# Three products of 512 columns where there were two of 512 and two of 256, on weight parts placed 64 bytes further

## The chip, the cores and the metric

One core of one Trainium2 chip runs the kernel. The time is device time of one execution, in microseconds (us). Three runs of the kernel before gave 994.24, 994.9 and 995.12 us; their median is 994.9 us.

## The reference, cut to what matters

Two layers of a decoder trunk on a sequence of 256 positions and 1024 features, all float32. Each layer is a gated feed-forward network, a mixer, and a second feed-forward network:

```python
x = x + 0.5 * swiglu(rms_norm(x, ffn1_norm), ffn1_w_gate_up, ffn1_w_down)
h = rms_norm(x, mix_norm)
z = h @ w_in                      # u, q, k, v and two gates
y_pool = multiscale_pool(u, pool_w, pool_scale)
y_attn = moba_attention(q, k, v)  # q and k normed by head, with rotary positions
merged = gates[:, :, 0] * (y_pool @ w_branch_pool) + gates[:, :, 1] * (y_attn @ w_branch_attn)
x = x + merged @ w_out
x = x + 0.5 * swiglu(rms_norm(x, ffn2_norm), ffn2_w_gate_up, ffn2_w_down)
```

Nearly all of the work is in the products of activations with weights: 1024 by 5632 and 2816 by 1024 in each feed-forward network, 1024 by 4096 in `w_in`, and three smaller ones in the mixer.

## The kernel before, in words

**Products in parts.** Every float32 operand is split into two float32r parts, a high one and a low one (`hi` and `lo` of the weights; for activations the two stand beside each other in one tile). A product of two operands is then three products of parts: high by high, high by low, low by high. In this text a step is one block of 128 rows in the sum over features.

**Two ways to lay a product on TensorE.** In most of the kernel the weights are stationary: a block of 128 by 128 of `hi` is loaded, and 512 columns stream past it (the high and the low part of the activations for 256 positions), then the block of `lo` is loaded and 256 columns stream (the high part alone). `chain` writes such a pair of one 512-column and one 256-column product. In the mixer's branches and its last projection, and in the last eighth of the last network, `chain3` writes three of 256 columns.

In two functions the activations are stationary and the weights stream, so that the result has positions, not features, on the partitions. `tokens` (L686) makes q, k and v in this way: it is called three times a layer, and a call takes two units of weights, two halves of 128 positions, and four steps each, 16 steps in all. `by_tokens` (L555) makes a part of the first product of the three later feed-forward networks. That part goes by sums of quadrants of the operands with seven products instead of eight (`SUMS`, the forms "1" to "7" in `seven`); a form is one unit of weights and four steps. The list `TWO` has two groups of seven such forms, `THREE` has three groups and is used twice, so there are 8 groups and 56 forms. The stationary activations are blocks of `hx` for the forms "1", "2" and "4", and of a tile `sf` with their sums and differences for "3", "5", "6" and "7".

A step in these two functions has four products. `ah` and `al` are the high and low parts of a stationary block, `wh` and `wl` the high and low parts of 512 columns of weights, S is 256:

- 512 columns: `ah` with `wh`
- 256 columns: `ah` with the first half of `wl`
- 512 columns: `al` with `wh`
- 256 columns: `ah` with the second half of `wl`

For the forms "1", "2" and "4" in `by_tokens` the second and the third are exchanged. The same four add into one result of 512 columns.

**How columns are read.** `steps` (L218) reads the streaming operand in four rounds: in each round 4 elements (16 bytes) out of every 16 (64 bytes). The result is written in the same order. All products are recorded on one line, that of `mm` (L110); they are told apart by their tiles.

**Where the operands lie.** A unit of weights is one megabyte, and `buffers` (L202) takes one `raw` tile and two `hi` and two `lo` tiles of 1024 elements each (4096 bytes a partition). There are four `raw` buffers and six each of `hi` and `lo`; the six of one name lie behind one another. Tiles of a multiple of 128 bytes keep the same residue modulo 128 throughout, so `hi`, `lo`, `hx` and the other tiles of parts share one. The tile `sf` (L533) is longer than its content and begins SHIFT, 16 elements or 64 bytes, further in, so it is 64 bytes off the weights that stream past it.

**What sets the order.** SP's queue brings the weights in the order of a plan written out by hand; `unit` takes the next pair of parts and `fetch` (L134) starts the next unit: a DMA into `raw`, the high part by ACT (L209, or L198 for units made of quadrants, in `sum_form`, L187), and the low part by DVE (L210 or L199). A `raw` buffer comes free when DVE has read it, a part's buffer when TensorE has read it. POOL's queue makes sums of quadrants in memory beforehand. TensorE runs its products in the order in which they are written (`keep`). The first six units of each layer's `w_in` (q, k and v, two each) are those that `tokens` takes.

Of the kernel before, what the change touches and what calls it, by code (L numbers as in the profile page):

```python
# [19 lines left out]
F32R = mybir.dt.float32r  # L20
# [5 lines left out]
P = 128  # L26
D = 1024
S = 256
L = 2
NK = D // P  # L30
DFF = 2816
NF = DFF // P
# [6 lines left out]
HALF = 8 * P  # L39
# [6 lines left out]
LU = FU + NF + NF // 2  # L46
GROUPS = {"A": 12, "B": 8, "C": 18}
XF = 2
SHIFT = 16
# [29 lines left out]
def trunk_kernel(ctx: ExitStack, tc: tile.TileContext, x_in, w_in, pw_in, qkn_in, rope_in, mask_in, band_in, out):  # L79
# [4 lines left out]
    parts = ctx.enter_context(tc.tile_pool(name="parts", bufs=6))  # L84
# [24 lines left out]
    def mm(*args, **kw):  # L109
        return keep(nc.tensor.matmul(*args, **kw))  # L110
# [17 lines left out]
    def unit():  # L128

        if not ahead:  # L130
            fetch()
        return ahead.pop(0)

    def fetch(last=None):  # L134

        u = next(plan)
        if isinstance(u, tuple):
            ahead.append(sum_form(*u))
            return
        raw, hi, lo = buffers()  # L140
        n = HALF if u < 4 else 2 * HALF
        for c in range(0, 2 * HALF, n):
            nc.sync.dma_start(raw[:, c:c + n], w_in[u, :, c:c + n])
        for h in range(2):
            low = split(raw[:, h * HALF:(h + 1) * HALF], hi[h], lo[h])
        if last:
            behind(low, last)
        ahead.append((hi, lo))
# [3 lines left out]
    def quadrant(base, g, q):  # L152

        n, kh = base + GROUPS[g] + (0 if q[1] == "1" else 2), int(q[0]) - 1
        return w_in[n:n + 2, :, kh * HALF:(kh + 1) * HALF].rearrange("u p c -> p u c")

    def two_rows(z):
        return z.rearrange("p (i c) -> p i c", i=2)
# [28 lines left out]
    def sum_form(base, n):  # L187

        f, g = n
        z, hi, lo = buffers()  # L190
        src = quadrant(base, g, RAW[f]) if f in RAW else two_rows(far.pop((f, g, base)))
        z = two_rows(z)
        nc.sync.dma_start(z, src)
        z = z.rearrange("p i (k c) -> p i k c", c=2 * P)
        for h in range(2):
            a = z[:, :, 2 * h:2 * h + 2, :]
            hv, lv = (t[h].rearrange("p (k i c) -> p i k c", i=2, c=2 * P) for t in (hi, lo))
            act(hv, a, AF.Copy)  # L198
            tt(lv, a, hv.bitcast(F32), op=OP.subtract)  # L199
        return hi, lo  # L200

    def buffers():  # L202
        raw = raws.tile([P, 2 * HALF], F32, name="raw", tag="raw")
        hi = [parts.tile([P, HALF], F32R, name="hi", tag="hi") for _ in range(2)]
        lo = [parts.tile([P, HALF], F32R, name="lo", tag="lo") for _ in range(2)]
        return raw, hi, lo

    def split(w, hi, lo):
        act(hi, w, AF.Copy)  # L209
        return tt(lo, w, hi.bitcast(F32), op=OP.subtract)  # L210

    def blk(z, b, n=1):

        size = z[0].shape[-1]
        c = b * P % size
        return z[b * P // size][:, c:c + n * P]

    def steps(z):  # L218

        if len(z.shape) == 3:  # L220
            z = z.rearrange("p a s -> p (a s)")
        return z.rearrange("p (s a c) -> p a s c", a=4, c=4)

    def prod(ps, w, xk, first, last, **kw):

        return mm(steps(ps), lhsT=w, rhs=steps(xk), start=first, stop=last, **kw)
# [35 lines left out]
    def behind(z, other):  # L262

        tc.add_manual_dep(z.ins, other.ins.name, mybir.DependencyInfo(
            mybir.DependencyClass.NoSync, mybir.DependencyReason.DATA), reason="behind")
# [46 lines left out]
    hx = acts.tile([P, NK, 2, S], F32R, name="hx")  # L312
# [83 lines left out]
    def eight(dtype, name, at=0):  # L396
        z = acts.tile([P, NK * GW + 4 * SHIFT], dtype, name=name, tag="gates")[:, at:]
        return [z[:, i * GW:(i + 1) * GW] for i in range(NK)]
# [21 lines left out]
    def ffn(after, n0=0, end=False, col=None, base=0, far_at=(), steps_at=()):  # L420
        gs, gt = {}, {}

        def room(name, n0, m):
            g = acts.tile([P, m, 2, S], F32R, name=name, tag=name)
            gt[name] = g
            gs.update({n0 + i: g[:, i] for i in range(m)})
# [9 lines left out]
        abs_, more = {}, []  # L436
# [59 lines left out]
        else:  # L496
# [24 lines left out]
            sf = {}  # L521
# [3 lines left out]
            def x_forms():  # L525

                late = drained[-1]
                for k in range(NK):
                    behind(act(xg[:, k, :], x[:, k, :], AF.Copy, scale=gain[:, l_of[0], col + k:col + k + 1]), late)
                (a11, a21), (a12, a22) = ([z[:, :, t * P:(t + 1) * P] for t in range(2)] for z in (xg[:, :4], xg[:, 4:]))  # L530
                s1, s2 = (pre[:, (8 + 2 * i) * S:(10 + 2 * i) * S].rearrange("p (k s) -> p k s", s=P) for i in range(2))
                s3, s4 = (vt[:, i, :].rearrange("p (k s) -> p k s", s=P) for i in range(2))
                fs = iter(eight(F32R, "sf", SHIFT))  # L533

                def parts_of(n, z):
                    sh, sl = (next(fs).rearrange("p (k s) -> p k s", s=P) for _ in range(2))
                    act(sh, z, AF.Copy)
                    tt(sl, z, sh.bitcast(F32), op=OP.subtract)
                    sf[n] = [(sh[:, k, :], sl[:, k, :]) for k in range(4)]

                tt(s3, a11, a21, op=OP.subtract)
                parts_of("7", s3)
                yield
                tt(s1, a22, a21, op=OP.subtract)
                stt(s2, s1, -1.0, a11, op0=OP.mult, op1=OP.subtract)
                parts_of("6", s2)
                yield
                parts_of("5", s1)
                yield
                stt(s4, s2, -1.0, a12, op0=OP.mult, op1=OP.subtract)  # L550
                parts_of("3", s4)
                room("gb", 16, NF - 16)
                yield

            def by_tokens(f, ps, first):  # L555

                hi, lo = unit()
                more = {} if first else {"skip_group_check": True}
                for k, (ah, al) in enumerate(sf[f]):
                    wh, wl = blk(hi, 4 * k, 4), blk(lo, 4 * k, 4)  # L560
                    low = ps[:, :S], ah, wl[:, :S], False, False
                    prod(ps, ah, wh, first and k == 0, False, **more)
                    if f not in "124":
                        prod(*low, **more)
                    prod(ps, al, wh, False, False, **more)
                    if f in "124":
                        prod(*low, **more)
                    prod(ps[:, S:], ah, wl[:, S:], False, k == 3, **more)
                fetch()

            def gated(c, t, n, sign):
# [54 lines left out]
            for n in FEED[base][2:]:  # L626
                next(xf, None)
                if isinstance(n, str):
                    (turned if n[0] == "t" else seven)(*((int(n[1]), n[2]) if n[0] == "t" else n))
                    continue  # L630
                n, t = n if isinstance(n, tuple) else (n, None)
                pair(unit(), wide(n), *([lambda: turned(int(t[1]), t[2]), NK // 2] if t else ()))
                fetch()
                if n in steps_at:
                    go_on()
                if n == XF:
                    xf = x_forms()
                    for _ in xf if not three else "":
                        pass
                if n % 2 and n > 1:  # L640
                    post(wait[0])
                    wait = [n - 1, n]
# [5 lines left out]
        for f, k in order:  # L648
            u, c = divmod(f * NF + k, 16)
# [4 lines left out]
            hi, lo = parts_of[u]  # L654
            if k == 0:
                sums_of[f] = quarter("ps")
            ps = sums_of[f]
# [28 lines left out]
    def tokens():  # L686

        pt = pmm.tile([P, 2, GW], F32, name="pt", tag="mm")
        for kh in range(2):
            hi, lo = unit()  # L690
            for t in range(2):
                ts = slice(t * P, (t + 1) * P)
                for kk in range(4):
                    k = kh * 4 + kk
                    wh, wl = blk(hi, 4 * kk, 4), blk(lo, 4 * kk, 4)
                    prod(pt[:, t], hx[:, k, 0, ts], wh, k == 0, False)
                    prod(pt[:, t, :S], hx[:, k, 0, ts], wl[:, :S], False, False)
                    prod(pt[:, t], hx[:, k, 1, ts], wh, False, False)
                    prod(pt[:, t, S:], hx[:, k, 0, ts], wl[:, S:], False, k == NK - 1)
        return pt  # L700

    def normed(pt, rt, name):
# [91 lines left out]
    def mix(l, after):  # L794
# [235 lines left out]
        for step in ((0, 0, 6), (1, 0, 6), (2, 0, 6), (0, 6), (1, 6), (2, 6), *((f,) for f in range(3, NK))):  # L1030
            project(*step)

    w3 = [buffers() for _ in range(3)]
    parts3 = eight(F32R, "p3", 2 * SHIFT)
    w3.append((raws.tile([P, 2 * HALF], F32, name="raw", tag="raw"), parts3[:4], parts3[4:]))
    done = 0
    for f in range(0, NK, 2):
# [3 lines left out]
        for u, (raw, hi, lo) in enumerate(w3):  # L1041
            nc.sync.dma_start(raw[:, 2 * f * P:2 * (f + 2) * P], w_in[u, :, 2 * f * P:2 * (f + 2) * P])
            n = 1 if f == 0 else 2
# [114 lines left out]
```

## Time and profile before

| What | Value |
|---|---|
| Median of three runs | 994.9 us (994.24 to 995.12) |
| Span of the profiled execution | 991.9 us |
| Instructions | 16162, of them 6296 matmuls |
| TensorE busy | 986.1 us, 99% |
| VectorE (DVE) busy | 811.2 us, 82% |
| ScalarE (ACT) busy | 661.6 us, 67% |
| DMA moved | 285.19 MB, 288 GB/s on average |
| Granted clock of TensorE | 0.999 |

The page gives the span of the profiled execution, from its first instruction to its last, and no total of its own beside it; the runs of the table lie 2.3 to 3.2 us above that span. A row of the groups has the line, the engine and operation, what is written and read, the shape and the count; behind the first bar the busy time and the mean time of one in ns, behind the second the engine's idle time just before. A row of the timeline has the start and the duration in us. A row of the chain of waits has the start and the length of a piece in us, its engine and line, and the number of instructions in it. PE is TensorE's matmul, PEld its weight load. Matmuls overlap, so the time that one takes from the next is the distance of their starts and not their duration.

### The profile page before, as it was taken

Reading aid. Unit: us, or ns where it says so; the run is one execution under the profiler, and the core shown is the slowest. Engines: PE = TensorE matmul, PEld = TensorE weight load, DVE = VectorE, ACT = ScalarE, POOL = GpSimd, SP = SyncE. Lnnn points to the kernel's source line nnn. Section 1 sums busy time; section 2 is a strip of 40 time slices with the busy share of each in tenths; the row PEclk is TensorE's granted clock in tenths of the full one; section 3 lists DMA queues with packets and bytes.
Section 4 is the critical chain, followed back from the end, with each engine's and each line's share of the span. In section 5 each row is a group of like instructions: output and inputs, shape, how many; then the busy total and the mean of one; then the engine's idle time right before and its main releaser. Section 6 shows DMA issues by size and latency. Waiting matters only on the chain.

```text
span 991.9 us, 16162 instructions
## 1 busy us (share of the span) xinstructions
PE 986.1 (99%) x6296; PEld 895.4 (90%) x6296; DVE 811.2 (82%) x1154; ACT 661.6 (67%) x988; POOL 71.0 (7%) x111
## 2 busy tenths in 40 slices
PE   9999999999999999999999999999999999999998
PEld 8989888898899988889888889988988998888897
DVE  6987777698978798886779999776988887999872
ACT  7865555567766787775578877555677568887641
POOL 0000010104100000000000000000141000000000
PEclk9999999999999999999999999999999999999999
DMA  8889899989979769899979989898799998988840
GB/s 298 322 297 323 254 327 343 309 241 292 323 237 328 255 242 324 297 325 286 311 267 305 321 289 347 277 311 279 258 298 372 248 306 299 320 314 292 293 150 22
DMA packets 50269, 285.19 MB, mean 288 GB/s; under 512 B 4753, under 2 KB 6033, under 8 KB 27409
## 3 DMA queue, kind: packets, MB, share of 16 engines
q1 hardware_dynamic: 36624, 217.05, 58.8%
q0 software_dynamic: 13568, 67.11, 27.7%
q8 instruction: 49, 0.80, 0.3%
q14 instruction: 28, 0.22, 0.1%
HBM read 283.10 MB, written 68.16 MB: 354 GB/s over the span
## 4 chain that ended last, share of the span: by engine, by line
PE 99%; DMA 0%; DVE 0%; ACT 0%; SPq 0%; issue 0%
PE ps L110 68%; PE b L110 15%; PE pt L110 7%; PE two L110 4%; PE pe L110 1%; PE sc L110 1%; PE pt L780 1%; PE y L110 1%; PE b L588 0%; DMA raw<-w 0%; PE tp L736 0%; PE pt L588 0%; PE st L110 0%; PE ss L110 0%; DVE t L681 0%; ACT hi L209 0%
## 5 line engine op out<-in xcount | busy, mean ns | idle before, releaser
L210 DVE TENSOR_TENSOR lo<-raw,hi 128x1024 fp32r<-128x1024 f32 (+2 forms) x303 | 360.9, 1203 | 104.3 <-ACT hi L209 102.9
L209 ACT ACTIVATE hi<-raw 128x1024 fp32r<-128x1024 f32 (+2 forms) x303 | 310.6, 1033 | 194.8 <-PE ps L110 123.1
L110 PE MATMUL ps<-hx,hi 128*128 128x512 f32 x1184 | 400.2, 384 | 0.6 <-ACT hi L209 0.6
L110 PE MATMUL ps<-hx,lo 128*128 128x256 f32 x1184 | 323.7, 273 | 0.0
L110 PEld LDWEIGHTS ps<-hx,hi 128*128 128x128 f32 x1184 | 222.2, 188 | 40.7 <-ACT hi L209 0.8
L110 PEld LDWEIGHTS ps<-hx,lo 128*128 128x128 f32 x1184 | 222.5, 188 | 0.3 <-DVE lo L210 0.3
L199 DVE TENSOR_TENSOR lo<-raw,hi 128x1024 fp32r<-128x1024 f32 x112 | 135.0, 1220 | 17.7 <-ACT hi L198 17.5
L198 ACT ACTIVATE hi<-raw 128x1024 fp32r<-128x1024 f32 x112 | 117.5, 1056 | 41.4 <-PE ps L110 25.3
L110 PE MATMUL ps<-ga,hi 128*128 128x512 f32 (+1 forms) x264 | 87.8, 378 | 0.0
L110 PE MATMUL b<-hi,sf 128*128 128x512 f32 x256 | 87.4, 383 | 0.0
L183 POOL DMA_DIRECT2D f<-w x48 | 44.6, 932 | 557.7 <-DVE ab L259 239.4
L110 PE MATMUL b<-lo,sf 128*128 128x256 f32 x256 | 70.2, 274 | 0.0
L110 PE MATMUL ps<-ga,lo 128*128 128x256 f32 x256 | 69.9, 273 | 0.0
L110 PE MATMUL ps<-gb,hi 128*128 128x512 f32 (+1 forms) x198 | 65.4, 376 | 0.0
L110 PE MATMUL pt<-hi,hx 128*128 128x512 f32 x192 | 64.9, 384 | 0.0
L110 PE MATMUL b<-hi,hx 128*128 128x512 f32 x192 | 59.1, 388 | 0.0
L110 PEld LDWEIGHTS ps<-ga,hi 128*128 128x128 f32 x264 | 49.0, 188 | 8.2
L110 PEld LDWEIGHTS b<-hi,sf 128*128 128x128 f32 x256 | 48.0, 188 | 8.4
L110 PE MATMUL pt<-lo,hx 128*128 128x256 f32 x192 | 52.5, 274 | 0.0
L110 PE MATMUL ps<-gb,lo 128*128 128x256 f32 x192 | 52.4, 273 | 0.0
L110 PEld LDWEIGHTS ps<-ga,lo 128*128 128x128 f32 x256 | 48.1, 188 | 0.0
L110 PEld LDWEIGHTS b<-lo,sf 128*128 128x128 f32 x256 | 48.0, 188 | 0.0
(209 smaller groups left out, 1590.6 us busy)
## 6 DMA issues: line engine op xcount, KB each, us to landing
raw<-w SPq DMA_DIRECT2D x168, 1024.0 KB, 7.2
f<-w POOLq DMA_DIRECT2D x48, 1024.0 KB, 11.9
raw<-f SPq DMA_DIRECT2D x32, 1024.0 KB, 5.8
raw<-w SPq DMA_DIRECT2D x16, 256.0 KB, 5.3
out_dram<-gx SPq DMA_DIRECT2D x8, 128.0 KB, 1.9
gx<-x SPq DMA_DIRECT2D x3, 256.0 KB, 5.5
qk<-pw SPq DMA_DIRECT2D x2, 256.0 KB, 5.7
gx<-x SPq DMA_DIRECT2D x1, 300.0 KB, 2.8
```

Source lines behind the costliest of these rows:

```text
L110: return keep(nc.tensor.matmul(*args, **kw))
L183: z = nc.gpsimd.dma_start(two_rows(far[f, g, base]), src, **kw)
L198: act(hv, a, AF.Copy)
L199: tt(lv, a, hv.bitcast(F32), op=OP.subtract)
L209: act(hi, w, AF.Copy)
L210: return tt(lo, w, hi.bitcast(F32), op=OP.subtract)
L780: keep(nc.tensor.transpose(pt[:, h, o * P:(o + 1) * P], pr[:, h, c * P:(c + 1) * P], ident))
```

## The change

In `by_tokens` and `tokens` each step has three products of 512 columns: `ah` with `wh`, `al` with `wh`, `ah` with `wl`. The two halves of `wl` are no longer apart, and all forms have the same order. The sums are the same.

Each `hi` and `lo` tile gets 2 x SHIFT more elements (128 bytes a partition). The parts of the units that stream in these two functions (all of `sum_form`, and the first six units of each layer's `w_in`) start 64 bytes into their tiles, the others at the start. The content of `sf` starts 128 bytes into its tile, so it stays 64 bytes off those weights; `hx` stays where it was, so it is now 64 bytes off them too.

```diff
@@ fetch
-        raw, hi, lo = buffers()
+        t = (u - NF - NF // 2) % LU
+        raw, hi, lo = buffers(SHIFT if t < 6 else 0)
@@ sum_form
-        z, hi, lo = buffers()
+        z, hi, lo = buffers(SHIFT)
@@
-    def buffers():
+    def buffers(at=0):
         raw = raws.tile([P, 2 * HALF], F32, name="raw", tag="raw")
-        hi = [parts.tile([P, HALF], F32R, name="hi", tag="hi") for _ in range(2)]
-        lo = [parts.tile([P, HALF], F32R, name="lo", tag="lo") for _ in range(2)]
+        hi, lo = ([parts.tile([P, HALF + 2 * SHIFT], F32R, name=n, tag=n)[:, at:at + HALF] for _ in range(2)]
+                  for n in ("hi", "lo"))
         return raw, hi, lo
@@ x_forms
-                fs = iter(eight(F32R, "sf", SHIFT))
+                fs = iter(eight(F32R, "sf", 2 * SHIFT))
@@ by_tokens
-                    low = ps[:, :S], ah, wl[:, :S], False, False
                     prod(ps, ah, wh, first and k == 0, False, **more)
-                    if f not in "124":
-                        prod(*low, **more)
                     prod(ps, al, wh, False, False, **more)
-                    if f in "124":
-                        prod(*low, **more)
-                    prod(ps[:, S:], ah, wl[:, S:], False, k == 3, **more)
+                    prod(ps, ah, wl, False, k == 3, **more)
@@ tokens
                     prod(pt[:, t], hx[:, k, 0, ts], wh, k == 0, False)
-                    prod(pt[:, t, :S], hx[:, k, 0, ts], wl[:, :S], False, False)
                     prod(pt[:, t], hx[:, k, 1, ts], wh, False, False)
-                    prod(pt[:, t, S:], hx[:, k, 0, ts], wl[:, S:], False, k == NK - 1)
+                    prod(pt[:, t], hx[:, k, 0, ts], wl, False, k == NK - 1)
```

## The prediction

> **What bounds the kernel now.** I read the head of the page first, then its chain of work that ended last, then the waits of TensorE alone, and only then single matmuls.
>
> ```profile
> span 991.9 us, 16162 instructions
> PE 986.1 (99%) x6296; PEld 895.4 (90%) x6296; DVE 811.2 (82%) x1154; ACT 661.6 (67%) x988; POOL 71.0 (7%) x111
> PEclk9999999999999999999999999999999999999999
> ...
> PE 99%; DMA 0%; DVE 0%; ACT 0%; SPq 0%; issue 0%
> ...
> PE busy L110 <- DVE eps L298: 1.1, 1, 1.1
> PE ps L110 <- ACT hi L209: 0.6, 1, 0.6
> ```
>
> TensorE is busy from end to end at full clock, 99% of the chain is its own, and its waits for anybody sum to 1.7 us, both at the start. So the time is a sum of matmuls, and a change to the matmuls is worth exactly what it does to the distance from one matmul's start to the next. The durations in the groups (384 ns for 512 columns, 273 for 256) overlap and don't add up; starts do. The chain of waits in order of time gives long pieces of one kind with their counts, and those divide well:
>
> ```profile
> 215.99 10.67 PE ps L110 x64
> 284.27 19.26 PE two L110 x168
> ```
>
> The first is 32 pairs of one 512-column and one 256-column product: 10.67 / 32 = 333.4 ns a pair. The second is 168 products of 256 columns alone: 19.26 / 168 = 114.6 ns each. By difference a 512-column product costs 333.4 - 114.6 = 218.8 ns. Per column that is 104.2 / 256 = 0.407 ns, which leaves some 10 ns a product that doesn't depend on its width (218.8 - 512 x 0.407). That is what the change can save: the columns stay at 1536 a step, the products go from four to three.
>
> The work that it touches, by groups of one shape each:
>
> ```profile
> L110 PE MATMUL b<-hi,sf 128*128 128x512 f32 x256 | 87.4, 383 | 0.0
> L110 PE MATMUL b<-hi,hx 128*128 128x512 f32 x192 | 59.1, 388 | 0.0
> L110 PE MATMUL pt<-hi,hx 128*128 128x512 f32 x192 | 64.9, 384 | 0.0
> ```
>
> Each step has two wide products, so there are 128 steps with sf stationary, 96 with hx in `by_tokens` and 96 in `tokens`: 320 steps, 1280 products now and 960 after. A unit in `by_tokens` is four steps: 32 units with sf, 24 with hx. In `tokens` 16 steps make one call, six calls in all.
>
> **What they cost now.** One unit of each sort in the timeline of TensorE, from its first start to the first start behind it (the first and last rows of each):
>
> ```profile
> 336.73 0.61 PE L110 MATMUL b<-hi,hx 128*128 128x512 f32 x2
> 337.19 0.39 PE L110 MATMUL b<-lo,hx 128*128 128x256 f32 x2
> 337.41 0.61 PE L110 MATMUL b<-hi,hx 128*128 128x512 f32 x2
> 337.87 0.39 PE L110 MATMUL b<-lo,hx 128*128 128x256 f32 x2
> 338.10 0.62 PE L110 MATMUL b<-hi,hx 128*128 128x512 f32 x2
> 338.55 0.39 PE L110 MATMUL b<-lo,hx 128*128 128x256 f32 x2
> ...
> 339.46 0.68 DVE L259 TENSOR_TENSOR ab<-ps,ab 128x512 f32<-128x512 f32 x1
> ...
> 358.20 0.38 PE L110 MATMUL b<-hi,sf 128*128 128x512 f32 x1
> 358.42 0.28 PE L110 MATMUL b<-lo,sf 128*128 128x256 f32 x1
> 358.54 0.38 PE L110 MATMUL b<-hi,sf 128*128 128x512 f32 x1
> ...
> 360.88 0.38 PE L110 MATMUL ps<-hx,hi 128*128 128x512 f32 x1
> ```
>
> With sf: 358.20 to 360.88 is 2.68 us a unit. With hx three steps of four are seen: 336.73 to 337.41 to 338.10, 0.685 a step, so 2.73 a unit. The longer pieces of the chain agree, and give `tokens` too:
>
> ```profile
> 518.94 5.49 PE b L110 x32
> 535.11 5.36 PE b L110 x32
> ...
> 182.24 10.72 PE pt L110 x64
> 193.30 10.78 PE pt L110 x64
> 204.44 10.68 PE pt L110 x64
> 671.74 10.96 PE pt L110 x64
> 683.04 10.78 PE pt L110 x64
> 694.17 10.68 PE pt L110 x64
> ```
>
> 518.94 is two units with hx (2.745 each), 535.11 two with sf (2.68 each). The six calls of `tokens` are 64.6 us. The whole: 24 x 2.73 + 32 x 2.68 + 64.6 = 65.5 + 85.8 + 64.6 = 215.9 us.
>
> These rows also show what the placing does. A step of four at the pair price is 2 x 333.4 = 667 ns, so a unit would be 2.667. The sf units, whose stationary operand lies 64 bytes off the weights (modulo 128), are 13 ns above that; the hx units, which lie on the same residue and have their wide products back to back, are 65 above it, and there a wide product goes by 0.46 / 2 = 0.23 us (336.73 to 337.19; 0.46 and 0.45 in the next two steps, mean 228 ns). And one call of `tokens`, with the same code and the same residue as the other five, took 10.96: 342.5 ns a pair, 9 above the settled price, all the way through. So there is a settled and an unsettled way in which loads and streams interleave, and the residue of 64 seems to help it settle.
>
> **The price that isn't in the trace** is that of a wide product behind a wide product at a distance of 64 bytes. Bounds: 218.8 ns from below (the difference above), 228 from above (back to back at the same residue). I take 220: the start distance of a wide product in the sf unit (358.20 to 358.42), which has the distance of 64 that all have afterwards, and a narrower product behind it should not make the wide one itself quicker or slower. To each unit and call I add the 13 ns of settling that the sf units show.
>
> - Units with hx: 12 x 0.220 + 0.013 = 2.653; 24 x (2.73 - 2.653) = 1.8 us saved.
> - Units with sf: 32 x (2.68 - 2.653) = 0.9 us saved. Their distance to the weights is 64 before and after (sf moves with them), so only the count of products changes.
> - `tokens`: 288 x 0.220 + 6 x 0.013 = 63.4; two calls of 10.78 carry 0.1 of waiting at their start (10.78 against 10.68), which stays: 63.6; 1.0 us saved.
>
> Together 3.7 us.
>
> A rule speaks of the first price. The Trainium skill, "TensorE: Matmul & The Clock Gate", section "Back-to-back issue gap", gives a warm product alone as N / 2.4 + 2.5 ns, for 512 columns some 216 ns. By that figure the sum would be 960 x 4 ns = 3.8 us lower still, an estimate from the page; the trace's 218.8 and 220 don't bear it out for this strided stream.
>
> **What costs nothing.** 320 weight loads go too. A load starts with the product before the one that it serves:
>
> ```profile
> 358.42 0.19 PEld L110 LDWEIGHTS b<-hi,sf 128*128 128x128 f32 x1
> 358.54 0.19 PEld L110 LDWEIGHTS b<-lo,sf 128*128 128x128 f32 x1
> ```
>
> The load issued at 358.42 serves the product that starts at 358.54, so it lies under the narrow product at 358.42; after the change each has a wide product as cover, twice the room. If that cover failed a load could show with up to 0.19 us, but no start distance in these rows is longer for it. What a load might cost is already in the start distances.
>
> The splits by ACT and DVE keep their sizes and only write 64 bytes further on; their price there is not in the trace. The tightest place that I found between a split and its reader is this:
>
> ```profile
> 356.52 1.22 DVE L199 TENSOR_TENSOR lo<-raw,hi 128x1024 fp32r<-128x1024 f32 x1
> ...
> 359.77 0.27 PE L110 MATMUL b<-lo,sf 128*128 128x256 f32 x1
> ```
>
> Written at 357.74, read at 359.77: 2.0 us ahead. A unit becomes 0.03 to 0.08 us shorter, and the low part is read third instead of second, so neither eats that lead; a split would have to take over twice its 1.22 us first, and then TensorE would wait in `by_tokens`. Feeds: SP, ACT, DVE and POOL issue the same number of DMAs and instructions in the same order, and no wait is added. The buffers are handed back at the end of a unit as now.
>
> **The sum.** The chain is TensorE's, so 3.7 us come off the span: 991.9 to 988.2. The three runs are 994.24 to 995.12, 2.3 to 3.2 us above that span for what lies around it; from their median, 994.9 - 3.7 = 991.2 us. About 0.2% (2 us) is what a measurement of this kernel can tell from no change.
>
> **Rivals.**
>
> *The products never settle.* If back-to-back wide products keep colliding at a distance of 64, each goes at the 228 ns of the hx units: 960 x 8 ns = 7.7 us more than my sum, 4.0 above the time before, 998.9 us. The place is every step of `by_tokens` and `tokens`; it turns a loss from 224 ns a product on. For it: all back-to-back wide products in the trace are at about 228, and both units with 64 bytes alternate wide and narrow. Against it: the hx units differ in residue too, and `tokens` at that residue mostly runs settled. Beside it stands a rule of the Trainium skill, same page, "Step-by-step: what each phase is for": the load has its own SBUF read port and takes nothing from the stream. By it the 64 bytes would change nothing, and this rival would hold; the one call of 10.96 among five of 10.7 shows that something besides the code matters.
>
> *Halfway.* Some units settle and some don't, as the calls of `tokens` do: 222 to 226 ns on average is a saving of 1.8 us to a loss of 2.0, no change that can be told; centre 994.9.
>
> *Settled at the lower bound or better.* 218.8 ns takes another 1.2 us: 990.0. At the page's 216 it would be 987.4.
>
> *The rest is upset.* The part tiles get 128 bytes longer, so neighbours in the pool no longer lie on one residue modulo 256, and the feature-major products use the same tiles.
>
> ```profile
> 30.23 152.00 PE ps L110 x912
> L110 PE MATMUL ps<-hx,hi 128*128 128x512 f32 x1184 | 400.2, 384 | 0.6 <-ACT hi L209 0.6
> ```
>
> They now run settled: 152.00 / 456 = 333.3 a pair. If every second tile fell to the 342.5 of the bad call, 592 pairs x 9.1 = 5.4 us: 996.6. Against it: the residue modulo 128, which seemed to matter, is not changed there.
>
> **Chances.** The forecast 0.50; lower bound or better 0.10; halfway 0.20; never settles 0.13; the rest upset 0.07. Faster 0.60, same 0.20, slower 0.20. The range goes from 988.5, half into the better case, to 997.5, past the upset rest and most of halfway, leaving out the full price of never settling: about 0.8.
>
> **What would show it.** Products in `by_tokens` and `tokens`: 960 of 128x512, none of 256. Two sf units or two hx units in a row should both be near 5.31 us in the chain, a call of `tokens` near 10.6. Start distances of 0.22 prove the price, 0.23 the first rival. Pieces of `ps` should still divide to 333.4 a pair; if not, it is the last rival. TensorE's waits should stay under 2 us; if they grow, the feed was closer than its 2.0 us lead says.

## The result, and the profile after

The changed kernel takes 1004.75 us (median; 1004.31 to 1004.93), the one before 994.57 us beside it. The ratio is 1.010, 95% interval 1.0086 to 1.0114: 10.2 us slower, where 3.7 us faster was forecast.

The head of the page after, its chain by engine, and TensorE's own waits:

```profile
span 1003.0 us, 15530 instructions
PE 996.5 (99%) x5976; PEld 884.2 (88%) x5976; DVE 811.5 (81%) x1154; ACT 661.0 (66%) x988; POOL 70.9 (7%) x111
PEclk9999999999999999999999999999999999999999
...
PE 99%; DMA 0%; DVE 0%; ACT 0%; SPq 0%; issue 0%
...
PE ps L110 <- ACT hi L210: 1.2, 1, 1.2
PE busy L110 <- DVE eps L299: 1.1, 1, 1.1
```

There are 320 matmuls and 320 weight loads fewer (5976 for 6296), the clock is the same, TensorE's two waits, both at the start, grew only from 1.7 to 2.3 us in all, and yet it is busy 10.4 us longer. So it isn't a feed that ran late: products became dearer. The chain of waits in order of time, after, shows which (start, length, engine and line, number of products):

```profile
31.05 154.44 PE ps L110 x912
185.49 10.93 PE pt L110 x48
196.75 10.91 PE pt L110 x48
208.00 10.75 PE pt L110 x48
219.63 10.82 PE ps L110 x64
288.25 19.25 PE two L110 x168
525.50 5.44 PE b L110 x24
541.78 5.40 PE b L110 x24
```

Two things happened. The first row is the first feed-forward network, whose code the change doesn't touch: 456 pairs of 512 and 256 columns, 154.44 us for 152.00, or 338.7 ns a pair for 333.3. The row of 64 products at 219.63 took 10.82 for 10.67. And the products that were changed didn't gain what was forecast: two units with hx are 5.44 us (24 wide products, 226.7 ns each) where they were 5.49, two with sf 5.40 (225 ns) where they were 5.36, and the first three calls of `tokens` 32.59 where they were 32.18. The 256-column products of the branches (288.25) stayed at 114.6 ns.

To divide the whole, I summed the distances from one product's start to the next over the trace, by sort. Pairs are the 512- and 256-column products with stationary weights, with the few small float32r products of the norms; branches are the three 256-column products of `chain3` in the mixer.

| Sum of start distances, us | before | after | difference |
|---|---|---|---|
| pairs | 646.0 | 654.7 | +8.7 |
| `by_tokens`, hx | 65.6 | 65.5 | -0.1 |
| `by_tokens`, sf | 86.2 | 87.3 | +1.1 |
| `tokens` | 64.6 | 65.1 | +0.5 |
| branches and last projection | 88.4 | 88.7 | +0.3 |
| plain float32 products | 35.6 | 36.2 | +0.6 |

The differences add up to 11.1 us, as much as the two profiled spans differ (1003.0 and 991.9 us); by the medians it is 10.2. The 0.6 of the last row is the longer wait for the first split at the start (1.2 us for 0.6).

With the addresses that the two programs were built with, the wide products of the pairs in the trace after fall into two classes. Where the block being loaded meanwhile starts 128 modulo 256 bytes from the start of the stream, as all did before, a wide product takes 222.8 ns (918 of them); where it starts 0 modulo 256, it takes 228.6 (922). Tiles of 4096 + 128 bytes put every second buffer of `hi` and `lo` into the second class.

### The profile page after: what moved, and what is told of

The parts are those of the page before. It is cut to its first block, busy times and chain, and to the rows that moved or that the text cites. A ratio compares the mean times of both kernels' runs of the same rounds, so it can differ in the third digit from the quotient of the medians.

```text
span 1003.0 us, 15530 instructions
## 1 busy us (share of the span) xinstructions
PE 996.5 (99%) x5976; PEld 884.2 (88%) x5976; DVE 811.5 (81%) x1154; ACT 661.0 (66%) x988; POOL 70.9 (7%) x111
## 4 chain that ended last, share of the span: by engine, by line
PE 99%; DMA 0%; DVE 0%; ACT 0%; SPq 0%; issue 0%
PE ps L110 68%; PE b L110 15%; PE pt L110 7%; PE two L110 4%; PE pe L110 1%; PE sc L110 1%; PE pt L775 1%; PE y L110 1%; PE b L584 0%; DMA raw<-w 0%; PE tp L731 0%; PE pt L584 0%; PE st L110 0%; PE ss L110 0%; DVE t L677 0%; ACT hi L210 0%
## 5 line engine op out<-in xcount | busy, mean ns | idle before, releaser
L110 PE MATMUL ps<-hx,hi 128*128 128x512 f32 x1184 | 405.5, 388 | 1.2 <-ACT hi L210 1.2
L110 PEld LDWEIGHTS ps<-hx,hi 128*128 128x128 f32 x1184 | 222.1, 188 | 45.9 <-ACT hi L210 1.4
L110 PE MATMUL ps<-ga,hi 128*128 128x512 f32 (+1 forms) x264 | 88.7, 381 | 0.0
L110 PE MATMUL b<-hi,sf 128*128 128x512 f32 x256 | 78.8, 388 | 0.0
L110 PE MATMUL pt<-hi,hx 128*128 128x512 f32 x192 | 58.9, 387 | 0.0
L110 PE MATMUL b<-lo,sf 128*128 128x512 f32 x128 | 49.6, 387 | 0.0
L110 PE MATMUL ps<-gd,hi 128*128 128x512 f32 (+1 forms) x132 | 44.9, 380 | 0.0
L110 PE MATMUL ps<-gc,hi 128*128 128x512 f32 (+1 forms) x132 | 44.7, 379 | 0.0
```

## The experiments

Theory A: the place of the load against the stream, modulo 256 bytes, sets what the pairs cost, and the 128 bytes of added length spoilt it. Rival, theory B: the unsettled wide products (back to back in the changed steps) or the shifted starts upset the pairs behind them. And apart from that: do three wide products cost less than two wide and two narrow at all?

Four kernels, beside the kernel before at 994.31 us.

**Tiles longer by 256 bytes, in the changed kernel.** To make room the two small tiles `ca` and `cb` share a buffer.

```diff
-        hi, lo = ([parts.tile([P, HALF + 2 * SHIFT], F32R, name=n, tag=n)[:, at:at + HALF] for _ in range(2)]
+        hi, lo = ([parts.tile([P, HALF + 4 * SHIFT], F32R, name=n, tag=n)[:, at:at + HALF] for _ in range(2)]
...
-        ca = small.tile([P, 2, DH], F32, name="ca", tag="ca", bufs=1)
-        cb = small.tile([P, 2, DH], F32, name="cb", tag="cb", bufs=1)
+        cab = small.tile([P, 2, 2, DH], F32, name="cab", tag="sq", bufs=2)
+        ca, cb = cab[:, 0], cab[:, 1]
```

> The changed kernel, with part tiles 256 bytes longer than at first instead of 128 (the small tiles ca and cb share a buffer with sq to make room), so that neighbours in the pool lie on one residue modulo 256 again, as before the change. The 64 bytes and the three products stay. Theory A (a load whose block starts 0 modulo 256 from the stream unsettles the pairs of 512 and 256): pieces of ps go back to 333.4 ns a pair, 8.7 us come back; the back-to-back wide products stay near 227 ns, 1.5 us above before; about 996.1 us. Theory B (the unsettled wide products, or the shifted starts, upset the pairs that follow them): the pairs stay near 338, 1003 to 1005 us.

Measured: 994.43 us, ratio 1.0002 (0.9993 to 1.0011), no difference from before. Its chain of waits:

```profile
32.63 152.02 PE ps L110 x912
184.65 10.88 PE pt L110 x48
195.87 10.99 PE pt L110 x48
207.19 10.87 PE pt L110 x48
218.94 10.68 PE ps L110 x64
521.69 5.43 PE b L110 x24
537.80 5.37 PE b L110 x24
```

The pairs are back at 152.02 / 456 = 333.4 ns. (This execution began its first network 2.4 us later than that of before, 32.63 for 30.23, and 2.1 us of that lie in its first 16 products, which took 5.27 us for 3.17; behind them the pairs of the trace sum to 0.3 us less than before.) So 256 for 128 in one number takes away the whole loss: theory A. Summed over the trace, the wide products of `tokens` and of hx remain at 227.2 ns, but those of sf fall to 223.2 (5.37 / 24 = 223.8 in the row above), where the expectation had all of them near 227 and 996.1 us. Three products and the 64 bytes, with the pairs left in peace, are worth nothing: the changed steps cost 216.6 us, before 216.4.

**Tiles longer by 128 bytes, in the kernel before.** Nothing else: four products, content at the start.

```diff
-        hi = [parts.tile([P, HALF], F32R, name="hi", tag="hi") for _ in range(2)]
+        hi = [parts.tile([P, HALF + 2 * SHIFT], F32R, name="hi", tag="hi")[:, :HALF] for _ in range(2)]
```

The `lo` tiles are made alike.

> The kernel before, with nothing changed but part tiles that are 128 bytes longer (content at the start). Theory A: every second tile lies 0 modulo 256 from hx and the other streams, the pairs cost 8 to 9 us more, and the four-product steps some 1 to 2 us more for the half of their tiles that lies badly: 1003 to 1006 us. Theory B: no wide products back to back with shifted weights, so nothing changes: 994.6 us.

Measured: 1005.07 us, ratio 1.0109 (1.0094 to 1.0125), as slow as the changed kernel with the instruction list of the fast one.

```profile
31.14 154.44 PE ps L110 x912
185.58 10.95 PE pt L110 x64
219.95 10.85 PE ps L110 x64
```

The first row has the same 154.44 as the changed kernel. Summed, the pairs cost 654.9 us, 8.9 more than before; the steps of `by_tokens` and `tokens` 2.0 more. Theory B would have left this at 994.6.

**Three products in the kernel before, nothing moved.** The diff of the change in `by_tokens` and `tokens` alone.

> The kernel before, with three products of 512 columns and nothing moved: no longer tiles, no 64 bytes for the weights, sf 64 bytes off as before. Theory A: pairs at 333.4 as before; wide products back to back 226 to 228 ns wherever they lie, so 960 of them cost 217 to 219 us against 216.4 for the 1280 of before: 995 to 997 us. If the 64 bytes do help the wide products of hx, these are dearer here than the 227.4 ns of the changed kernel (228 to 235), 996 to 999 us. If fewer products do pay and only the placing spoilt it, 991 to 993 us.

Measured: 998.12 us, ratio 1.0033 (1.0019 to 1.0046).

```profile
31.10 152.00 PE ps L110 x912
183.10 11.50 PE pt L110 x48
194.94 11.13 PE pt L110 x48
521.60 5.74 PE b L110 x24
538.03 5.38 PE b L110 x24
```

The pairs are settled. Two units with hx went from 5.49 to 5.74, 239 ns for a wide product; the mean over all hx units is 231.6, over `tokens` 231.2, over sf (which has its 64 bytes) 224.4. So three products alone lose 3 us by the sums, and the 64 bytes win those back: hx falls from 231.6 to 227.2 in the first run, no further.

**Four products with the places of the first run.** The first run with the steps of before.

> The kernel of the 256-byte run with the four products of before, so that only the places differ from before: weights 64 bytes in, hx 64 bytes off them, one residue modulo 256. Theory A: pairs at 333.4; the steps of by_tokens and tokens as before or a little quicker, since all are now 64 bytes off: 993.5 to 995 us, and the difference to the 256-byte run with three products is the price of three against four at the same places. Theory B: if the shifted starts upset the pairs, above 1000 us.

Measured: 996.18 us, ratio 1.0017 (1.0008 to 1.0027).

```profile
32.33 152.02 PE ps L110 x912
184.35 10.78 PE pt L110 x64
195.47 10.88 PE pt L110 x64
```

Pairs settled; the shifted starts upset nothing. The time is above the 993.5 to 995 that was expected, though: the steps, which were to be as before or quicker, cost 217.7 us. By the medians three products at these places (994.43) are 1.75 us cheaper than four, by the sums of the two traces 1.1 (216.6 for 217.7), but four at the places of before are as cheap as three here. So the count has a price only together with the place.

Four more asked whether a better place exists, beside the kernel before at 994.18.

**Every load of the changed products at 192 modulo 256.** The weights start 192 bytes in, sf at the start of its tile; the rest is as in the first run, with tiles 256 bytes longer.

```diff
-        raw, hi, lo = buffers(SHIFT if t < 6 else 0)
+        raw, hi, lo = buffers(3 * SHIFT if t < 6 else 0)
-        z, hi, lo = buffers(SHIFT)
+        z, hi, lo = buffers(3 * SHIFT)
-                fs = iter(eight(F32R, "sf", 2 * SHIFT))
+                fs = iter(eight(F32R, "sf"))
```

> Three products and tiles 256 bytes longer as in the 256-byte run, but the streamed weights start 192 bytes into their tiles and sf at the start of its own, so that every load of by_tokens and tokens lies 192 modulo 256 from the stream (hx lay at 64 there, sf at 192). Theory A in its finer form (the price of back-to-back wide products goes by the residue modulo 256: 231 at 128, 227 at 64, 223 at 192): hx falls from 227 to about 223, 960 x 223.3 = 214.4 us against 216.4 of before, pairs at 333.4: 992 to 992.6 us, a little quicker than both kernels. Rival (sf is quicker than hx for another reason, such as which tile it is): hx stays at 227, 994.4 us.

Measured: 995.1 us, ratio 1.0007 (0.9998 to 1.0015): no gain, where theory A in its finer form had 992 to 992.6. Its chain, then its timeline in one call of `tokens`, first the beginning and then a later part:

```profile
30.44 152.00 PE ps L110 x912
182.45 10.78 PE pt L110 x48
```

```profile
182.29 0.61 PE L110 MATMUL pt<-hi,hx 128*128 128x512 f32 x2
182.74 0.40 PE L110 MATMUL pt<-lo,hx 128*128 128x512 f32 x1
182.98 0.63 PE L110 MATMUL pt<-hi,hx 128*128 128x512 f32 x2
183.44 0.39 PE L110 MATMUL pt<-lo,hx 128*128 128x512 f32 x1
183.67 0.60 PE L110 MATMUL pt<-hi,hx 128*128 128x512 f32 x2
...
185.02 0.61 PE L110 MATMUL pt<-hi,hx 128*128 128x512 f32 x2
185.47 0.39 PE L110 MATMUL pt<-lo,hx 128*128 128x512 f32 x1
185.70 0.61 PE L110 MATMUL pt<-hi,hx 128*128 128x512 f32 x2
186.14 0.38 PE L110 MATMUL pt<-lo,hx 128*128 128x512 f32 x1
186.36 0.61 PE L110 MATMUL pt<-hi,hx 128*128 128x512 f32 x2
```

The entry of a call and its settled stream both show here. The first two steps take 0.69 us each; later ones 1.34 / 2 = 0.67 (185.02 to 186.36). Over the last three quarters of each call it is 223.4 ns a product: 670 a step. That is a settled stream of wide products at this place, with the pairs at 128, and it is no cheaper than the 667 of a settled step of four. But sf rose from 223.2 in the first run to 226.5, at the same distance from the weights: so the residue isn't all. What came before counts as well, and a unit of 12 products is mostly entry, that is, beginning that hasn't settled yet.

**Four products at those places.**

> The run before this with the four products of before. By the settled price of a step of four (667 ns and 13 ns of settling a unit) 320 steps cost 214.5 us against 216.4: 992.4 us, as quick as three products at the same places, since three at 223 make 669. If a narrow product costs some 7 to 10 ns for itself wherever it lies, as the prediction had it, this is 2 to 3 us slower than the run with three: 994 to 995 us.

Measured: 996.07 us, ratio 1.002 (1.001 to 1.0029). The steps cost 216.2 us in its trace, three cost 216.9 in the run above, so the two are alike there as the first expectation had it; the pairs are 3.6 us dearer in this trace (of an execution 2 us above the median), 2.0 of them in the first 16 products (5.14 us for 3.17) and 1.6 behind these, and by the medians the kernel is 1 us slower. The second expectation isn't borne out in the steps; where in the rest the pairs lost 1.6 us is open.

**Pairs at 192, and pairs at 64.** All other parts also start 64 (or 192) bytes in.

```diff
-        raw, hi, lo = buffers(3 * SHIFT if t < 6 else 0)
+        raw, hi, lo = buffers(3 * SHIFT if t < 6 else SHIFT)
```

That is for 192, against the run with three products at 192; for 64 the argument is `3 * SHIFT` for all units.

> The three products at 192 as above, and besides the parts of all other units moved 64 bytes in, so that the pairs with stationary weights lie 192 modulo 256 from their streams instead of 128. If a settled pair costs 333.4 wherever it settles, 992 us as above. If 192 is the better place for pairs too, below 990. If only 128 lets pairs settle, each costs 337 to 340: 1000 to 1005 us.

> As the run before this with the pairs at 64 modulo 256 (all parts start 192 bytes in). By the wide products, which are dearer at 64 than at 192, the pairs should be no better than at 192: between 992 and 1005 us. At 0 (the changed kernel's odd tiles) they cost about 340.

Measured: 997.62 us, 1.004 (1.0027 to 1.0054), with the pairs at 192; 996.68 us, 1.0025 (1.0015 to 1.0035), at 64. One row of the first, then two of the second:

```profile
30.48 152.02 PE ps L110 x912
```

```profile
30.70 153.53 PE ps L110 x912
556.65 13.21 PE b L110 x60
```

At 192 the first long stretch settles as at 128 (152.02), but pairs in sum cost 2.2 us more and the branches 1.1; the time fits none of the three that were expected. At 64 they are at 153.53 / 456 = 336.7 ns, 5.9 us more in sum. There, and only there, the changed products won what the prediction hoped for: 13.21 / 60 = 220.2 ns each, 213.3 us in sum, 3.1 below before. The pairs around them give it back. Four products were not run beside such pairs, so how much of the 3.1 is due to the count isn't shown.

The second run also shows what the products before a unit do. With the pairs at 64, the changed products lie exactly where they lay in the run with three products at 192; only the pairs around them moved. Yet hx went from 226.2 to 221.3 ns a wide product and sf from 226.5 to 222.1. What runs ahead of a unit sets its price as much as its own place.

Then two of the kernel before, beside it at 994.63.

**All parts at 0 modulo 256**: 128 bytes into tiles 256 bytes longer.

```diff
-        hi = [parts.tile([P, HALF], F32R, name="hi", tag="hi") for _ in range(2)]
+        hi = [parts.tile([P, HALF + 4 * SHIFT], F32R, name="hi", tag="hi")[:, 2 * SHIFT:2 * SHIFT + HALF] for _ in range(2)]
```

The `lo` tiles are made alike, and `ca` and `cb` share a buffer as above.

> The kernel before, four products and all, with every hi and lo part 128 bytes further into tiles 256 bytes longer: each load of the pairs now lies 0 modulo 256 from its stream, where in the run with tiles 128 bytes longer half of them did (8.9 us in the pairs). Theory A: twice that, 16 to 19 us in the pairs, and the steps with hx stationary are at 0 too: 1012 to 1017 us. Rival (the mixture of two residues in turn is what unsettles, not the residue 0): all are alike again, 994 to 996 us.

Measured: 1009.79 us, ratio 1.0151 (1.0135 to 1.0166).

```profile
31.26 155.03 PE ps L110 x912
220.60 10.99 PE ps L110 x64
```

The rival falls: it is the residue 0, not the mixture. The pairs cost 12.9 us more, less than twice 8.9, so a change of residue from tile to tile costs something too (a wide product of a pair at 0 goes by 227.2 ns here, by 228.6 in the changed kernel), and the size expected was too large.

**One order for all forms.**

```diff
                     prod(ps, ah, wh, first and k == 0, False, **more)
-                    if f not in "124":
-                        prod(*low, **more)
+                    prod(*low, **more)
                     prod(ps, al, wh, False, False, **more)
-                    if f in "124":
-                        prod(*low, **more)
```

> The kernel before with one order for all forms in by_tokens: wide, narrow, wide, narrow for the forms 1, 2 and 4 as well, which have two wide and then two narrow products. Nothing is moved. If back-to-back wide products are what keeps these 24 units from settling, each falls from 2.73 to 2.67 or 2.68: 1.2 to 1.5 us, 992.8 to 993.2 us. If the place of hx (128 modulo 256, and at first the same tile) decides, no change, 994.3 us.

Measured: 995.71 us, ratio 1.0009 (1.0001 to 1.0018): no gain, by its sum 65.8 us for hx against 65.6. The back-to-back wide products were not what kept the hx units dear.

**Parts 32 and 16 bytes in**, otherwise as the run at 0 modulo 256, beside the kernel before at 994.39.

> The kernel before, four products, with every hi and lo part 32 bytes into tiles 256 bytes longer: pairs at 160 modulo 256, hx stationary at 96, sf at 160. It asks whether a place between 128 and 192 settles at less than 333.4 ns a pair. If steps of 64 bytes are the finest that matter, pairs cost as at 128 or at 192, and the time is 994 to 998 us. If the place within 64 bytes matters too, anything from 980 (pairs near 328, the smallest start distances seen, 219 and 109) to 1010.

> The same with 16 bytes: pairs at 144 modulo 256, hx stationary at 112, sf at 176. The streams read 16 bytes out of each 64 in a round, so this moves the load by one such word against the round. Same alternatives: 994 to 998 us if only steps of 64 bytes matter, 980 to 1010 if the word does.

Measured: 1001.57 us, ratio 1.0067 (1.0051 to 1.0084), with 32 bytes; 1006.08 us, 1.0118 (1.0103 to 1.0133), with 16. Three rows of the first, two of the second:

```profile
32.44 152.04 PE ps L110 x912
287.19 19.71 PE two L110 x168
452.69 61.16 PE ps L110 x358
```

```profile
30.74 154.61 PE ps L110 x912
288.62 19.04 PE two L110 x168
```

The 16-byte word matters too, and not in one direction: 16 bytes unsettle the pairs (339.1 ns) and make the branches quicker (19.04 / 168 = 113.3 ns), 32 bytes leave the first long stretch settled, but not a later one (61.16 us, before 59.67), and make the branches slower (117.3). No place that was tried is better for the whole than 128.

## Why the prediction was wrong

**What bounds the kernel** held: the time is the sum of the start distances, before and after, and the waits grew by 0.6 us alone, at the start. The lead of the splits, the feeds and the unchanged queues were rightly costed at nothing.

**The step that failed most is the last rival's "against it".** The prediction named the longer tiles, the place and the mechanism (every second tile on another residue modulo 256, settled pairs falling out of step), and then put it at 0.07 because "the residue modulo 128, which seemed to matter, is not changed there". The trace before had loads only at 128 and 192 modulo 256 in its long stretches, so it could say nothing of 0; not changed modulo 128 was no reason. The run with longer tiles and nothing else has the whole of it. The size, 5.4 us, was too small because the 592 pairs were counted in one group only; ga, gb, gc and gd stream past the same tiles. Half of all 1898 pairs at the same 9.1 ns would have been 8.6 us. Measured: 8.7 us.

**The price of a wide product behind a wide product** was taken as 220 ns, from a wide product with a narrow one behind it; over the changed kernel it is 227.4 (hx), 227.3 (sf) and 226.2 (`tokens`), near the upper bound of 228, and the term of 3.7 us saved became 1.5 us lost. Of that loss 1.3 us are the long tiles again: with tiles 256 bytes longer the mean is 225.6 ns and the loss 0.2 us. So of the 13.6 us between the 991.2 forecast and the result, this price has 3.2 (to the 994.43 of that run) and the long tiles the other 10.3. Settled at 192 it is 223, and 220 came only beside pairs at 64. The 220 was one start distance; over all 256 wide products of the sf units the same trace has 223.2, entries included. The reason given for it, that the narrow product behind it should make no difference, holds nearly for sf (224.4 with three products and nothing moved) and fails for `tokens`, 223.6 before and 231.2 there.

**Some 10 ns for each product whatever its width** failed with it. It came from 333.4 and 114.6 by difference, but the two belong to different streams: the 114.6 is of the branches. Within the pairs of the first network before, the starts give 221.3 ns for a wide product and 112.1 for a narrow one, which leaves 3 ns. Settled at 192, three wide products take 670 ns a step, and two wide with two narrow 667 at the pair price: there the smaller count saves nothing.

**That 64 bytes help to settle** held where three wide products follow one another (hx 231.6 without, 227.2 with), but the residue modulo 128 isn't the whole: 64 and 192 differ (`tokens` 227.2 and 224.7), and what came before counts.

**The rivals were priced as if only one could happen.** Never settling (+4.0) and the rest upset (+5.4) work at different places and can come together: the changed steps lost 1.5 us, the pairs 8.7. That 994.9 + 9.4 = 1004.3 lies so near the 1004.75 measured is luck, one term being too large and the other too small. They aren't independent either, since most of the 1.5 came with tiles 128 bytes longer; with tiles 256 bytes longer, at 994.43 us and 225.6 ns a wide product, the prediction's halfway rival is what came. The range held each alone, or nearly, and not their sum.

The Trainium skill ("TensorE: Matmul & The Clock Gate", section "Step-by-step: what each phase is for") has the loads on a port of their own that takes nothing from the stream. The two kernels with equal instruction lists, 994.31 and 1005.07 us, don't agree with that for these streams of 16 bytes out of 64: with the feeds unchanged, only the addresses differ. What in the memory collides was not seen.

Three things stay open. In the pairs only the weights were moved, never the streams, so it isn't shown whether the distance between the two sets the price or the weights' own address modulo 256. Nor is it shown why a unit of `by_tokens` at 192, with hx or with sf, needs some ten products to settle beside pairs at 128 and hardly any beside pairs at 64, and which part of an entry decides how a unit runs.

## What to carry to other kernels

In this kernel, where TensorE is the bound and reads 16 bytes out of every 64, the length of a buffer in a rotating pool is a parameter of speed: adding 128 bytes to it cost 1%, and 256 bytes left the pairs as they were. Before tiles are moved or lengthened, write down the residues of stationary and streaming operands modulo 256 for every user of the pool, not only for the products that the change is about. And when two rivals work at different places, ask what they cost together.

## What the runs showed of the hardware

The same instructions at other addresses differ by 1.5% of the whole: pairs of a 512- and a 256-column float32r product cost 333.4 ns with the load 128 modulo 256 from the stream, 336.7 at 64, 340.0 at 0 (155.03 / 456), 339.1 at 144, all in the first long stretch. The state has memory: at one place a call of `tokens` starts at 230 ns a wide product and ends at 223, and what a unit does depends on the products before it (226.2 ns beside pairs at 128, 221.3 beside pairs at 64, for hx at 192).
